# The down projection of a streaming encoder step computed from seven block products instead of eight

## The chip, the cores and the metric

The kernel runs on one core of one Trainium2 chip. The metric is the time of one execution on the device in microseconds (us). The engines are named as in the profile: PE does the matmuls (PEld loads their stationary operands), DVE, ACT and POOL do the work on vectors, SP issues most of the DMAs, and POOL issues some.

## The reference

One step of a one-layer encoder: a mixer of three kinds of recurrent heads, then a feed-forward block with a causal convolution. It works on 1024 prompt rows and 32 sample rows of 1024 features in float32. The change is in the second half:

```python
def conv_ffn(xn, buf, w_up, conv_w, conv_b, w_down):
    up = xn @ w_up                                   # 1024 -> 2 x 2816
    up, buf = causal_dwconv(up, buf, conv_w, conv_b) # width 3
    gate, val = jnp.split(up, 2, axis=-1)
    return (jax.nn.gelu(gate, approximate=True) * val) @ w_down, buf   # 2816 -> 1024
...
h, ffn_buf = conv_ffn(rms_norm(x, g_ffn_pre[l]), ...)
x = x + rms_norm(h, g_ffn_post[l])
```

The product `(gelu(gate) * val) @ w_down` is the down projection: 1056 rows x 2816 features x 1024 outputs. A post norm over the 1024 outputs and the residual follow.

## The kernel before

Every large product is taken in three matmuls of a split operand: `split` (lines 108 to 113) rounds a float32 tile to float32r on ACT (line 110) and takes the remainder on DVE (line 113); `mm3` (lines 103 to 106) adds high x high, high x low and low x high into one PSUM bank. So each operand tile costs one ACT cast and one DVE subtraction, whatever number of matmuls reads it.

The up projection (`up_all`) runs over 22 feature tiles `f` and over two halves `s` of the columns (the rows of the input, 528 columns each). For each it takes seven block products `p1` to `p7` of a 2 x 2 scheme (`up_block`), so it saves one product in eight already. `up_raw` loads the two weight tiles of the next `f` on SP. `up_finish` makes the convolution (POOL copies a few halo columns into `uu`, lines 1335 to 1338; ACT line 1339; DVE line 1341), the gelu (line 1343) and the product with the other half (line 1344), and stores the tile to `h_d[f]` in DRAM (line 1345), 128 features x 1060 columns: 512 prompt rows, two gap columns, 32 sample rows, two gap columns, 512 prompt rows. `uu` is a single pair of buffers. The tile framework orders the instructions of each engine by a timeline of its own and sets the semaphores.

The down projection (`down_all`) takes the 1056 rows in three groups (`DGROUPS`): row blocks 0, 1 and the sample rows (block 8); then 2, 3, 4; then 5, 6, 7. Each group goes over all 22 feature tiles: `load_h` loads the group's columns of `h_d[f]` and all of `w_dn[f]` (512 KB, so the weights are loaded three times) and splits both. Group 0 has the weights stationary and its 288 columns moving (8 banks; the result is turned by PE transposes, line 1460), the others have the rows stationary and 512 weight columns moving. `finish` takes the squares (ACT line 1421), multiplies by the gain (DVE line 1423), gets the reciprocal root on POOL and adds the residual (line 1429) before the store. The last four feature tiles of the last group are held back and done bank by bank, so that the row blocks finish one after the other. `ahead` begins the first two feature tiles of group 0 before the up projection has ended.

PSUM has 8 banks here: four of tag `xw` and one of `sx` in `psf`, three of `big` in `psb`. Split weights live in seven buffers of tag `op`, raw weights in two of tag `raw`.

Of the kernel before, what the change touches and what calls it, by code (L numbers as in the profile page):

```python
# [18 lines left out]
SEQ = 1024  # L19
# [19 lines left out]

DGROUPS = [(0, 1, 8), (2, 3, 4), (5, 6, 7)]  # L40

# [53 lines left out]
def body(ctx: ExitStack, tc: tile.TileContext, a: dict):  # L95
# [45 lines left out]
    h_d = dr.tile([NF, 128, NCOL], F32, name="h_d")  # L141

# [1076 lines left out]

    def up_raw(f):  # L1220
        res = []
        for j in (f, NF + f):
            r = praw[0].tile([128, 1024], F32, tag="raw", name=f"wu{j}r", bufs=2)
            sp.dma_start(r, a["w_up"][j].rearrange("p k n -> p (k n)"))
            res.append(r)
        return res
# [102 lines left out]
    def up_finish(py, f, uu):  # L1329

        ys = []
        for i, j in enumerate((f, NF + f)):
# [5 lines left out]
            pool.tensor_copy(fhalo[:, j, :], u[:, NCOL - 2:NCOL])  # L1338
# [8 lines left out]
    def up_all(pw_, W0, X, uus, py, ahead, begun):  # L1347

        raw, W = {}, {0: W0}
        late = None  # L1350
        for f in range(NF):
# [3 lines left out]
            for s in range(2):  # L1355
# [23 lines left out]
    praw = []  # L1379

    def load_h(ph, g, f, spans, w, deep=None):
        r = ph.tile([128, 384], F32, tag="hr", name=f"hr{g}_{f}", bufs=2)
        for (c0, c1, o) in spans:
            sp.dma_start(r[:, o:o + c1 - c0], h_d[f, :, c0:c1])
        hh = ph.tile([128, 384], F32R, tag="hh", name=f"hh{g}_{f}", bufs=4)
        hl = ph.tile([128, 384], F32R, tag="hl", name=f"hl{g}_{f}", bufs=4)
        split(hh[:, :w], hl[:, :w], r[:, :w], dve)
        wr = praw[0].tile([128, 1024], F32, tag="raw", name=f"wd{g}_{f}r", bufs=2)
        sp.dma_start(wr, a["w_dn"][f])
        return hh, hl, [weight_halves(f"wd{g}_{f}{hf}", wr[:, 512 * hf:512 * hf + 512], deep) for hf in range(2)]  # L1390

    def spans_of(us):
        spans, off, w = [], {}, 0
        for u in us:
            n = 128 if u < 8 else DEC
            off[u] = w
            if spans and spans[-1][1] == fcol(u):
                spans[-1][1] += n
            else:
                spans.append([fcol(u), fcol(u) + n, w])  # L1400
            w += n
        return spans, off, w

    def down_all(ph, p6, gp, begun):
        xres = {}

        def residual(u):
            n = 128 if u < 8 else DEC
            x = p6.tile([128, 1024], F32, tag="xres", name=f"fr{u}", bufs=4)
            sp.dma_start(x[:n], x2_d[128 * u:128 * u + n, :])  # L1410
            xres[u] = x

        def finish(u, n, src):

            x = xres.pop(u)
            ss = p6.tile([128, 4], F32, tag="fss", name=f"gss{u}", bufs=4)
            jk = p6.tile([128, 1024], BF16, tag="fjk", name=f"gjk{u}", bufs=2)
            ys = []
            for hf in range(2):
                c = slice(512 * hf, 512 * hf + 512)  # L1420
                act.activation(jk[:n, c], src[hf], AF.Square, accum_out=ss[:n, 2 + hf:3 + hf])  # L1421
                y = p6.tile([128, 512], F32, tag="yt", name=f"yt{u}{hf}", bufs=4)
                dve.tensor_tensor(y[:n], src[hf], gp[:n, c], op=ALU.mult)
                ys.append(y)
            pool.tensor_tensor(ss[:n, 0:1], ss[:n, 2:3], ss[:n, 3:4], op=ALU.add)  # L1425
            rstd_of(ss[:n, 1:2], ss[:n, 0:1], n, 1, 1024)
            for hf in range(2):
                c = slice(512 * hf, 512 * hf + 512)
                dve.scalar_tensor_tensor(x[:n, c], ys[hf][:n], ss[:n, 1:2], x[:n, c], op0=ALU.mult, op1=ALU.add)
                sp.dma_start(a["yp"][128 * u:128 * u + n, c] if u < 8 else a["ys"][:, c], x[:n, c])  # L1430

        def banks_of(g, m):

            where = [(psf, "xw", 4)] * 4 + [(psb, "big", 3)] * 3 + [(psf, "sx", 1)]
# [330 lines left out]
```

## Time and profile before

| | us |
|---|---|
| median of 3 runs | 1408.08 (1407.53 to 1409.46) |
| the profiled execution's own time | 1407.89 |
| its span, first to last instruction | 1405.9 |
| PE busy | 1364.0 (97%) |
| DVE busy | 1013.9 (72%) |
| ACT busy | 710.8 (51%) |
| POOL busy | 287.9 (20%) |
| mean granted clock of PE | 0.988 of full speed |

A row of a timeline is: start, duration, engine, line, operation, output <- input, shapes, count, and in brackets the idle time of the engine before it and what ended that. A row of instruction groups has the busy time, the mean duration in ns and the idle time before. Matmuls are pipelined: their rows overlap, so their rate is read from start to start and not from durations. Lines L104 to L106 are the three matmuls of `mm3`, and L722 the helper through which the mixer's small products go.

### The profile page before, as it was taken

The page shows a single profiled execution, that of the slowest core. Times are in us where ns is not written, and L with a number is a line of the kernel's source. Part 1 is how long each engine was busy: PE and PEld are TensorE (multiplying, and loading weights), DVE is VectorE, ACT ScalarE, POOL GpSimd, SP SyncE. Part 2 cuts the span into 40 slices and gives each one's busy share as a digit, 9 for nine tenths or more (in the row PEclk, how much of TensorE's full clock was granted, in tenths as well). Part 3 has the DMA queues.
Part 4 walks back from the last instruction along what each step waited for, and adds up shares of the span by engine and source line. Part 5 has one row for each costly group of instructions (what it writes and reads, how often), then busy time and mean ns, then how long its engine had stood idle before and what let it go on. Part 6 is the DMA issues. An engine that isn't in the chain of part 4 may idle for free.

```text
span 1405.9 us, 30168 instructions
## 1 busy us (share of the span) xinstructions
PE 1364.0 (97%) x11804; PEld 1249.8 (89%) x11804; DVE 1013.9 (72%) x1907; ACT 710.8 (51%) x1399; POOL 287.9 (20%) x495
## 2 busy tenths in 40 slices
PE   6999999999999999999899999999999999999998
PEld 5999889898888887777799999999999999988886
DVE  4786468758587669777798888888888865654644
ACT  4556447445474545334755555455545545543432
POOL 5532311235112245212111111111111110000100
PEclk9999999999999989999999999999999999999999
DMA  9599779775789744445312222222122267765752
GB/s 344 191 338 359 259 237 306 230 271 196 270 270 353 249 154 139 142 135 145 124 58 92 97 85 69 84 79 89 62 91 77 74 201 235 242 218 165 252 173 101
DMA packets 129445, 255.11 MB, mean 181 GB/s; under 512 B 27639, under 2 KB 74263, under 8 KB 129303
## 3 DMA queue, kind: packets, MB, share of 16 engines
q1 hardware_dynamic: 122839, 244.54, 52.5%
q10 hardware_dynamic: 4800, 4.33, 0.9%
q0 software_dynamic: 1664, 4.33, 0.8%
q8 instruction: 92, 1.51, 0.4%
q14 instruction: 50, 0.41, 0.1%
HBM read 192.26 MB, written 60.89 MB: 180 GB/s over the span
## 4 chain that ended last, share of the span: by engine, by line
PE 76%; DVE 9%; DMA 7%; ACT 4%; issue 2%; POOL 1%; SPq 0%; ACTq 0%; DVEq 0%; POOLq 0%
PE pd L104 6%; PE pd L105 6%; PE pd L106 6%; PE pux L104 4%; PE pux L105 4%; PE pux L106 4%; PE puw L106 3%; PE puw L104 3%; PE puw L105 3%; PE pv L106 2%; PE pv L104 2%; PE pv L105 2%; PE zp L104 2%; PE zp L106 2%; PE zp L105 2%
## 5 line engine op out<-in xcount | busy, mean ns | idle before, releaser
L1341 DVE SCALAR_TENSOR_TENSOR y<-uu,fconv_sb,y 128x1060 f32<-128x1060 f32 x88 | 116.2, 1321 | 25.0 <-ACT y L1339 24.3
L105 PE MATMUL pd<-wd,hh 128*128 128x512 f32 x264 | 104.3, 395 | 0.0
L104 PE MATMUL pd<-wd,hh 128*128 128x512 f32 x264 | 104.1, 396 | 0.0
L106 PE MATMUL pd<-wd,hl 128*128 128x512 f32 x264 | 104.0, 395 | 0.0
L1277 ACT COPY c<-pux 128x272 f32<-128x272 f32 (+1 forms) x132 | 49.2, 375 | 41.3 <-PE pux L106 37.6
L1339 ACT ACTIVATE y<-uu,fconv_sb 128x1060 f32<-128x1060 f32 x44 | 56.2, 1276 | 17.1 <-POOL uu L1335 16.5
L104 PE MATMUL pv<-wt_0h,xh 128*128 128x256 f32 (+2 forms) x195 | 57.8, 296 | 5.5 <-ACT xh L323 4.5
L104 PE MATMUL zp<-woh,ch 128*128 128x512 f32 (+1 forms) x144 | 58.9, 411 | 1.9 <-DVE z L1158 1.2
L105 PEld LDWEIGHTS pd<-wd,hh 128*128 128x128 f32 x264 | 49.5, 187 | 12.0
L106 PEld LDWEIGHTS pd<-wd,hl 128*128 128x128 f32 x264 | 49.5, 187 | 12.0
L104 PEld LDWEIGHTS pd<-wd,hh 128*128 128x128 f32 x264 | 49.5, 188 | 11.9
L106 PE MATMUL zp<-woh,cl 128*128 128x512 f32 (+1 forms) x144 | 57.6, 401 | 0.2 <-DVE cl L1054 0.2
L105 PE MATMUL zp<-wol,ch 128*128 128x512 f32 (+1 forms) x144 | 57.6, 400 | 0.0
L106 PE MATMUL pv<-wt_0h,xl 128*128 128x256 f32 (+2 forms) x195 | 56.7, 291 | 0.4 <-DVE xl L324 0.4
L106 PE MATMUL pv<-wt_1h,xl 128*128 128x256 f32 (+2 forms) x195 | 57.0, 292 | 0.0
L105 PE MATMUL pv<-wt_1l,xh 128*128 128x256 f32 (+2 forms) x195 | 56.8, 291 | 0.0
L104 PE MATMUL pv<-wt_1h,xh 128*128 128x256 f32 (+2 forms) x195 | 56.7, 291 | 0.0
L105 PE MATMUL pv<-wt_0l,xh 128*128 128x256 f32 (+2 forms) x195 | 56.2, 288 | 0.1
L1338 POOL COPY fhalo<-uu 128x2 f32<-128x2 f32 x44 | 17.6, 399 | 186.7 <-DVE uu L1282 186.7
L1425 POOL TENSOR_TENSOR gss<-gss 128x1 f32<-128x1 f32 (+1 forms) x9 | 2.2, 246 | 244.2 <-ACT gjk L1421 244.2
L104 PE MATMUL pd<-hh,wd 128*128 128x288 f32 x176 | 51.9, 295 | 0.0
L105 PE MATMUL pd<-hl,wd 128*128 128x288 f32 x176 | 51.9, 295 | 0.0
(1680 smaller groups left out, 5213.1 us busy)
## 6 DMA issues: line engine op xcount, KB each, us to landing
h_d<-y SPq DMA_DIRECT2D x22, 530.0 KB, 3.1
wt_0r<-in_w_tok SPq DMA_DIRECT2D x21, 512.0 KB, 5.3
wt_1r<-in_w_tok SPq DMA_DIRECT2D x21, 512.0 KB, 6.7
wt_0l<-lt_d SPq DMA_DIRECT2D x14, 512.0 KB, 3.9
wt_1l<-lt_d SPq DMA_DIRECT2D x14, 512.0 KB, 6.1
hr<-h_d SPq DMA_DIRECT2D x44, 128.0 KB, 3.4
hr<-h_d SPq DMA_DIRECT2D x22, 192.0 KB, 3.5
x<-in_xp SPq DMA_DIRECT2D x8, 512.0 KB, 8.8
```

What stands on the lines that cost most here:

```text
L104: pe.matmul(ps, lh[0], rh[0], start=first, stop=False, **kw)
L105: pe.matmul(ps, lh[0], rh[1], start=False, stop=False, **kw)
L106: return pe.matmul(ps, lh[1], rh[0], start=False, stop=last, **kw)
L1277: kept[name] = act.copy(t, ps)
L1338: pool.tensor_copy(fhalo[:, j, :], u[:, NCOL - 2:NCOL])
L1339: act.activation(y, u, AF.Identity, scale=fconv[:, j, 2:3], bias=fconv[:, j, 3:4])
L1341: dve.scalar_tensor_tensor(y, uu[i][:, s:s + NCOL], fconv[:, j, s:s + 1], y, op0=ALU.mult, op1=ALU.add)
L1425: pool.tensor_tensor(ss[:n, 0:1], ss[:n, 2:3], ss[:n, 3:4], op=ALU.add)
```

## The change

The 1024 prompt rows are cut into two halves, the 22 feature tiles into two halves of 11 (`NP`), the 1024 outputs into two halves. The four blocks of each factor and their sums give seven products `P1` to `P7` (Winograd's form), each over 11 feature pairs `p` with 512 rows, 128 features and 512 outputs a step: four row blocks x three matmuls of 512 columns. The products run in the order P2, P1, P4, P6, P5, P7, P3, in alternation in four banks `W` (`sx` and `big`) and four banks `X` (`xw`). Results are gathered in the SBUF tiles `CA` and `CB`.

- The row tiles `hts[f]` are loaded whole, once, and stay in SBUF, three of them (`EARLY`) during the last half tile of the up projection (`freed`), the others one or two with each step of P2 and one with each of P1 (`rows_of`). Their sums are taken in place on DVE (`combine`, `second_sum`, `fourth_sum`).
- The four sums of weight blocks are taken during the up projection in DRAM, in `ws_d`: 48 copies (`sum_weights`) of up to two feature tiles, 24 plain ones issued by SP behind the latest loads of up weights, and 24 that add to what is there, issued by POOL behind the latest `fhalo` copy. A sum's adding copy comes several copies after the one that it adds to.
- P1 and P2 load a whole tile of `w_dn` and split both halves, of which the product reads the first; the other products load one half or a sum, two feature tiles at a time.
- The 32 sample rows are multiplied in float32 (not split) from the raw tiles, during P2 and P1: with every second step four products (two feature tiles x two output halves) into four quarters of 32 partitions of one bank. Two products with a selection matrix `sel` add the quarters and bring them to the first 32 partitions.
- The gain's second half is negated, which gives the sign of one output half.
- One feature pair is begun ahead of the up projection's end, instead of two feature tiles.
- The last four pairs of P3 are held back and done bank by bank; the upper row blocks (4 to 7) are finished during P3's first steps.

The diff, cut to its core (the removed functions are printed above):

```diff
+    ws_d = dr.tile([4, 128, NF // 2, 512], F32, name="ws_d")
...
-            sp.dma_start(r, a["w_up"][j].rearrange("p k n -> p (k n)"))
+            behind["SP"] = sp.dma_start(r, a["w_up"][j].rearrange("p k n -> p (k n)"))
...
-            pool.tensor_copy(fhalo[:, j, :], u[:, NCOL - 2:NCOL])
+            behind["POOL"] = pool.tensor_copy(fhalo[:, j, :], u[:, NCOL - 2:NCOL])
...
                     next(late, None)
+                    if f == NF - 1 and s == 1:
+                        freed()
+                    m = (2 * f + s - 3) * len(SUMS) // 34
+                    while len(summed) < min(m, len(SUMS)):
+                        sum_weights(*SUMS[len(summed)])
+                        summed.append(m)
...
+    def sum_weights(t, n, q):
...
+        ta, tb, tc_, td = (ws_d[i, :, q:q + n] for i in range(4))
+        dst, x = ((ta, src(0, 0)), (tb, src(0, 1)), (ta, src(0, 1)), (tb, src(1, 1)), (tc_, ta),
+                  (tc_, src(1, 1)), (td, tc_), (td, src(1, 0)))[t]
+        plain = t in (0, 1, 4, 6)
+        with tc.issue_after(behind["SP" if plain else "POOL"].ins):
+            if plain:
+                sp.dma_start(dst, x)
             else:
+                pool.dma_start(dst, x, accum_op=ALU.add)
+    SUMS = [(t, min(2, NP - 2 * i), 2 * i) for _, t, i in
+            sorted((2 * i + 3 * t, t, i) for i in range((NP + 1) // 2) for t in range(8))]
...
+    def down_raw(kind, p):
...
+        turn[0] ^= 1
+        r = (ph[0] if turn[0] else praw[0]).tile([128, 2, 512], F32, tag="raw", name=f"wr{kind}_{p}", bufs=2)
...
+    def load_h(pool_, f):
+        hts[f] = pool_.tile([128, NCOL], F32, name=f"ht{f}")
+        with tc.issue_after(behind["SP"].ins):
+            sp.dma_start(hts[f], h_d[f])
...
+    ASRC = dict(P1=(0, 0), P2=(0, 1), P4=(1, 1), P6=(0, 0), P5=(1, 1), P7=(1, 0), P3=(0, 1))
...
+    def down_operands(ph, kind, p, early=False):
+        down_raw(kind, p)
+        h = halves_of(ablk(*ASRC[kind], p), f"{kind}h{p}", ph, "hop", 4)
+        wp = (ph, "hop", 4) if early else (praw[1], "op", 7)
+        if kind in ("P1", "P2"):
+            r = wraws[kind, p]
+            w = [halves_of(r[:, j], f"{kind}w{p}{j}", *wp) for j in range(2)]
+        else:
+            w = [halves_of(wraws[kind, p // 2][:, p % 2], f"{kind}w{p}", *wp)]
+        return h, w
+    def sample_products(ps, k, p):
+        for q in range(p - p % 2, p + 1):
+            for j in range(2):
+                r = 64 * (q % 2) + DEC * j
+                pe.matmul(ps[r:r + DEC], hts[q + NP * k][:, SMP:SMP + DEC], wraws["P2" if k else "P1", q][:, j],
+                          start=q < 2, stop=q >= NP - 2)
...
+        def run(kind, banks, first, last, each=None, n_end=0):
+            end = []
+            for p in range(NP):
+                ops = begun.pop((kind, p), None) or down_operands(ph, kind, p)
...
+                for i in range(4):
+                    c = slice(128 * i, 128 * i + 128)
+                    mm3(banks[i], (h[0][:, c], h[1][:, c]), wi, first and p == 0, last and p == NP - 1, skip_group_check=True)
+                if each:
+                    each(p, w)
+            return end
...
+        def rows_of(k, bank):
+            def each(p, w):
+                if p % 2 or p == NP - 1:
+                    sample_products(bank, k, p)
+                if k:
+                    for f in (NP + EARLY + p, p - NP + 6):
+                        if 0 <= f < NF and f not in hts:
+                            load_h(ph if f >= NP else ssp, f)
+                elif p + 6 < NP:
+                    load_h(ssp, p + 6)
...
+        run("P2", W, True, True, rows_of(1, s1))
...
+        run("P1", X, True, False, rows_of(0, s2))
...
+            pe.matmul(o[:DEC], sel[:, DEC * j:DEC * j + DEC], keep, start=True, stop=True)
...
+        run("P4", W, True, True, lambda p, w: combine(p))
...
+        close(8, DEC, y8, xs8, ss8)
+        second_sum(0)
+        run("P6", X, False, False, lambda p, w: p + 1 < NP and second_sum(p + 1))
...
+        run("P5", W, True, True, lambda p, w: fourth_sum(p))
...
+        run("P7", X, False, True)
...
+            dve.tensor_tensor(CB[:, i, 0], CB[:, i, 0], X[i], op=ALU.add)
+            dve.tensor_tensor(CB[:, i, 1], X[i], CB[:, i, 1], op=ALU.subtract)
...
+        end = run("P3", W, True, True, each, 4)
...
+    def freed():
+        pxs.close()
+        ph.append(phs.enter_context(tc.tile_pool(name="ph", bufs=1, side="left")))
+        down_raw("P2", 0)
+        for f in range(NP, NP + EARLY):
+            load_h(ph[0], f)
     def ahead():
+        for p in range(1):
+            begun["P2", p] = down_operands(ph[0], "P2", p, True)
```

More of the change, by code (lines that the diff above doesn't have):

```diff
@@ L1392, in spans_of @@
[L1392 to L1398, printed above, removed]
-            else:
[L1400 to L1424, printed above, removed]
@@ new lines, in down_all @@
+        W = w_banks("q5")
+        run("P5", W, True, True, lambda p, w: fourth_sum(p))
+        for i in range(4):
+            act.copy(CB[:, i, 1], W[i])
+            dve.tensor_tensor(CA[:, i, 1], CA[:, i, 1], W[i], op=ALU.subtract)
+        run("P7", X, False, True)
+        late.close()
+        px_ = late.enter_context(tc.tile_pool(name="p12", bufs=1, side="right"))
+        xres = {}
+        for u in (4, 5, 6, 7, 0, 1, 2, 3):
+            xres[u] = px_.tile([128, 1024], F32, name=f"fr{u}")
+            sp.dma_start(xres[u], x2_d[128 * u:128 * u + 128, :])
```

203 lines of the change are left out of this document (123 added, 80 removed).

## The prediction

> **What bounds the kernel now.** I read the page's busy line first, then the windows from the up projection to the end, then the timelines around the places that the change touches. Columns of the windows: length, then busy time and (x instructions) of PE, PEld, DVE, ACT, POOL, granted clock, DMA share, GB/s.
>
> ```profile
> PE 1364.0 (97%) x11804; PEld 1249.8 (89%) x11804; DVE 1013.9 (72%) x1907; ACT 710.8 (51%) x1399; POOL 287.9 (20%) x495
> 707.00:1140.00 433.00, 432.91 (x3549) 432.70 (x3548) 360.78 (x598) 223.53 (x388) 63.99 (x169) 1.00 0.24 82
> 1140.00:1156.00 16.00, 16.00 (x124) 16.00 (x123) 11.86 (x17) 7.59 (x12) 2.06 (x3) 1.00 0.89 279
> 1156.00:1212.00 56.00, 56.00 (x422) 56.00 (x422) 32.36 (x58) 28.78 (x58) 0.00 (x0) 1.00 0.76 235
> ...
> 1399.60:1405.90 6.30, 0.00 (x0) 0.00 (x0) 2.11 (x3) 0.69 (x2) 0.94 (x3) 0.77 0.22 83
> ```
>
> From 707 us on PE never waits, at full clock. DVE is at 83% in the up projection (360.78 of 433 us) and at 58% in the down projection (32.36 of 56), and DMA has most room in the up projection. So a product taken out of the down projection shortens the run, if its operands still arrive; the last 6.3 us are the tail of the last row block.
>
> **The products removed.** Now there are 528 matmuls of 288 columns and 792 of 512.
>
> ```profile
> L105 PE MATMUL pd<-wd,hh 128*128 128x512 f32 x264 | 104.3, 395 | 0.0
> L104 PE MATMUL pd<-hh,wd 128*128 128x288 f32 x176 | 51.9, 295 | 0.0
> 1299.64 0.40 PE L105 MATMUL pd<-wd,hh 128*128 128x512 f32 x1
> ...
> 1302.91 0.40 PE L104 MATMUL pd<-wd,hh 128*128 128x512 f32 x1
> 1140.26 0.30 PE L104 MATMUL pd<-hh,wd 128*128 128x288 f32 x1
> 1140.39 0.30 PE L105 MATMUL pd<-hl,wd 128*128 128x288 f32 x1
> ...
> 1141.86 0.28 PE L104 MATMUL pux<-T3h,S_21h 128*128 128x256 f32 x1
> ...
> 1143.28 0.29 PE L104 MATMUL pd<-hh,wd 128*128 128x288 f32 x1
> 1217.84 0.87 PE pt L1460 x8
> ```
>
> The rows overlap (395 ns each), so I count starts: 14 starts in 1302.91 - 1299.64 = 3.27 us, or 0.2336 us for 512 columns; 0.13 us for 288. The down projection starts at 1140.26 and its matmuls end at 1399.6: 259.3 us, with 1.4 us of interleaved up products (1141.86 to 1143.28) and three times 0.87 us for turning group 0. After: seven products x 11 feature pairs x 12 matmuls = 924 of 512 columns, 924 x 0.2336 = 215.8 us. By this alone the change saves about 42 us. What it gives back follows.
>
> **Sample rows.** 44 float32 matmuls, stationary 128x32, moving 128x512, in sets of four in four column quarters (per factor five sets of four and one of two: 12 sets).
>
> ```profile
> 365.31 0.29 PE L106 MATMUL pf<-xh,wf_8l 128*128 128x288 f32 x1
> 365.53 0.75 PE L548 MATMUL z<-r_fm,wg_sb 16*128 16x288 f32 x2
> 369.14 0.42 PE L722 MATMUL mi<-v,kt 128*32 128x64 f32 x12
> 587.60 0.39 PE L105 MATMUL zp<-wol,ch 128*128 128x512 f32 x1
> 587.92 0.27 PE L722 MATMUL mi<-ident,mqk 64*128 64x64 f32 x1
> 588.13 0.50 PE L106 MATMUL zp<-woh,cl 128*128 128x512 f32 x1
> 588.47 0.39 PE L104 MATMUL zp<-woh,ch 128*128 128x512 f32 x1
> ```
>
> The one product z is two records (x2): float32 is two passes. A 288-column float32r row lasts 0.29 us with 0.13 us between starts, so 0.16 us is latency; z's two passes stream for 0.75 - 0.16 = 0.59 us, about twice 2 x 0.13. So a 512-column pass is 2 x 0.2336 = 0.47 us and a sample product 0.93 us. Do quarters overlap? Twelve passes of 64 columns in 128*32 tiles would need 12 x 0.058 = 0.70 us in a row and take 0.42 - 0.16 = 0.26 us: three to four at a time. Going into another tile shape and back: one small product stretches 587.60 to 588.47, 0.87 us where two starts take 0.46, so at most 0.41 us, of which I take 0.36 as the switch. A set is 0.93 + 0.36 = 1.3 us, 12 sets 15.6 us. One after the other they cost 44 x 0.93 + 12 x 0.36 = 45 us: the other end. I take the low end, for the 128*32 row is the same tile shape.
>
> The Trainium skill's TensorE: Matmul & The Clock Gate (Part 3, measured speedup) gives three column tiles 2.38x. At that efficiency four would give an estimated 3.2x and a set 1.5 us; the sum would be 3 us higher.
>
> Then the halves are added (DVE), turned by two float32 products in one quarter (2 x 0.93 + 0.36 = 2.2 us), and PE waits for the DVE add (0.69 us by the L1423 row below, 1.4 us with an estimated 0.35 us for each of two hand-overs), since product four's first bank is the one that they use.
>
> **Operands per feature pair.** A pair lasts 12 x 0.2336 = 2.8 us on PE.
>
> ```profile
> 1057.02 0.69 DVE L113 TENSOR_TENSOR S_18h<-wu40r,S_18h 128x512 fp32r<-128x512 f32 x1
> 1057.62 0.69 DVE L1248 TENSOR_TENSOR wu18r<-wu40r,wu18r 128x512 f32<-128x512 f32 x1
> 1149.14 1.14 ACT L110 CAST wd<-wd_4r 128x512 fp32r<-128x512 f32 x2
> 1397.62 0.69 DVE L1423 TENSOR_TENSOR yt<-pd,gp 128x512 f32<-128x512 f32 x1 [0.27 <-ACT gjk L1421]
> 1395.94 1.41 DVE L1429 SCALAR_TENSOR_TENSOR fr<-yt,gss,fr 128x512 f32<-128x512 f32 x2 [0.49 <-POOL gss L223]
> ```
>
> A DVE operation of 512 columns takes 0.60 us from start to start, a cast on ACT 0.57. P2 and P1 still split the second weight half, which nothing reads: 3 x 0.60 = 1.8 of 2.8 us, free under PE. P4 has two splits and two row differences, 2.4 us, plus 2.4 us for the CA additions and about 3 us for the sample rows' finish: 32 us beside 31 of PE. Operands run up to three pairs ahead, so P4 itself loses nothing, but P6's first rows queue behind that finish: 2 us. P5, P6, P7 are below 2 us a pair. P3: eight CB additions, four upper row blocks at 2 x 0.60 + 1.41 us, four squares' products and the remaining seven pairs at 1.2 us give 4.8 + 10.4 + 2.4 + 8.4 = 26 us, then four times 2.6 us at the end: 36.4 us against 30.8 of PE and a tail of 7.3. The two nearly coincide; I take 2 us. The tail is 6.3 us and one DVE addition with its hand-over, 1 us. The other four changes of product find their banks already read: 0.5 us each, 2 us.
>
> **Start of the down projection.** Only one pair is begun ahead (2.8 us of PE) where two tiles of 24 matmuls were (6.4 us). DVE had 11.86 of 16 us to do at 1140 to 1156, mostly the last feature tile's convolution, and three splits a pair come to it. No cover is left: 3 us, between 0 and the 6.4 us.
>
> **Loads.** P2 loads 11 weight tiles of 512 KB and 14 row tiles of 530 KB, 13.4 MB in 31 + 8 = 39 us, 345 GB/s. The trace moved 279 GB/s at a share of 0.89, or 313 at a full share: 43 us. Three row tiles and one weight tile come before, so I take 2 us (0 to 15, rival three). The Trainium skill's DMA: Bandwidth & Descriptors (Specifications) puts a core's limit at about 358 GB/s, with which P2 would just fit: 2 us less.
>
> **Weight sums in the up projection.** 24 plain copies on SP, 24 adding copies from POOL, 512 KB each, some 25 MB in 350 us, 72 GB/s beside 82 at a share of 0.24: there is room even if an adding copy costs double. Each SP copy stands behind a pair of up loads, which have slack: wu19 is issued at 1060.81 and first used at 1070.35.
>
> ```profile
> 1050.51 0.33 SPq L1345 DMA_DIRECT2D h_d<-y  x1
> ...
> 1060.81 0.33 SPq L1224 DMA_DIRECT2D wu19r<-in_w_up  x1
> 1071.00 0.33 SPq L1345 DMA_DIRECT2D h_d<-y  x1
> 1070.35 0.62 ACT L110 CAST A_19h<-wu19r 128x512 fp32r<-128x512 f32 x1 [2.43 <-PE puy L106]
> L434 POOL DMA_DIRECT2D g_d<-vg x36: 537/582/792, 127.8 to 531.3; - x36
> 1063.76 0.19 POOL L1338 COPY fhalo<-uu 128x2 f32<-128x2 f32 x1 [3.53 <-DVE uu L1282]
> 1064.07 1.30 POOL L1335 COPY uu<-uu 128x2 f32<-128x2 f32 x1
> 1065.40 1.27 ACT L1339 ACTIVATE y<-uu,fconv_sb 128x1060 f32<-128x1060 f32 x1 [0.56 <-POOL uu L1335]
> ACT y L1339 <- POOL uu L1335: 16.5, 22, 2.2
> ```
>
> POOL is where it can hurt: the adding copies are queued behind the fhalo copy, and right behind that stands the uu copy for which ACT's y waits. An issue is 0.58 us. Behind a waiting adding copy stand all uu copies; but the copy that it adds to was issued several half tiles before (a tile's period is 1071.00 - 1050.51 = 20.5 us), so it should not wait. 24 x 0.58 = 14 us is the upper end if each delay reached PE, 0 the lower; y's users have some slack, and I take 1 us.
>
> **Sum.** From 1140.3: 1.4 up products + 215.8 + 15.6 + 2.2 + 1.4 + 2 (P6) + 2 (other changes) + 3 (start) + 2 (loads) + 2 (P3) + 7.3 (tail) = 254.7, span 1395.0; with 1 us in the up projection 1396.0. The profiled execution took 1407.89 us for a span of 1405.9, 2.0 us around it, and lies 0.2 us under the median of 1408.08: 1398.0 us.
>
> **Rivals.** One: the quarters don't overlap, because the scheduler puts float32r matmuls between them or different moving rows exclude each other. 45 - 15.6 = 29 us more: 1427. Against it stands the 128*32 row. It makes the run slower once a set takes over 2.1 us. Two: the adding copies hold up the uu copies and the up projection stretches, each time by an issue of 0.79 us, the longest seen: 24 x 0.79 = 19 us, 1416. It decides from 10 / 24 = 0.4 us per copy. For it: uu is one buffer, and ACT already waits there 22 times; against it: DVE is idle for 17% there, and the longest of those waits, 2.2 us, cost PE nothing. Three: loads bind P2: at the 235 GB/s of 1156 to 1212, 13.4 MB take 57 us, 15 to 18 more than PE, and the run ends at 1413; the share of 0.76 there, with PE fully busy, says that 235 was demand and not a limit.
>
> **Chances.** Forecast 0.70, with a range of its own of 1386 (start, loads, P6, the other changes, P3 and the up projection at nothing, 12 less) to 1408 (start at 6.4, sets 3 more, 4 in the up projection); rivals 0.08, 0.12 and 0.10. About 0.2% (2.8 us) is what can be told from no change here. Of the forecast 0.06 lies within that, of rival three 0.02; so faster 0.64, same 0.08, slower 0.28. The range takes in rivals two and three and leaves out one: 1386 to 1417.
>
> **What would show it.** Right: 924 products at 0.23 us starts; sample passes in fours, 1.3 us a set; up period still 20.5 us; PE gaps of 1 to 3 us at P2's start, before P4, before P6 and nowhere else. Wrong: up period over 21 us with waits on POOL uu; PE waiting on DMA for ht or wr in P2; DVE over 95% in P4 or P3 with PE idle beside it.

## The result and the profile after

The changed kernel takes 1404.97 us (median of 20 runs, 1401.84 to 1409.88) against 1409.27 us of the kernel before (20 runs beside it). The ratio is 0.997, with a 95% interval of 0.9959 to 0.998: faster, by 4.3 us, where the prediction had 10. The direction was right and the time lies in the range, but more than half of the gain is missing.

The profiled execution took 1408.66 us for a span of 1406.9 us, 3.7 us above the median. Executions differ ahead of the change: the first matmul of the up projection lay between 661.9 and 668.7 us in the profiled executions of kernels that are alike up to there. So stages are compared by their lengths below, not by the times at which they end.

The first line of the page after, then the windows of the profile after, cut at the stages. The columns are those of the windows in the prediction: length, busy time of PE, PEld, DVE, ACT and POOL, granted clock, DMA share, GB/s.

```profile
PE 1355.1 (96%) x11476; PEld 1208.4 (86%) x11476; DVE 1047.4 (74%) x1947; ACT 718.1 (51%) x1393; POOL 321.2 (23%) x519
```

```profile
668.70:1143.84 475.14, 468.03 (x3758) 463.48 (x3756) 390.59 (x633) 252.34 (x445) 88.96 (x209) 1.00 0.47 133
1143.84:1187.96 44.12, 44.12 (x185) 26.48 (x185) 30.27 (x47) 24.70 (x42) 2.03 (x3) 1.00 0.94 356
1187.96:1230.96 43.00, 42.40 (x181) 25.98 (x179) 25.86 (x42) 20.01 (x37) 0.00 (x0) 1.00 0.57 195
1230.96:1238.45 7.49, 3.53 (x6) 0.54 (x5) 7.49 (x14) 4.62 (x9) 0.00 (x0) 0.65 0.39 125
1238.45:1362.46 124.01, 124.01 (x529) 99.67 (x529) 80.40 (x130) 57.42 (x104) 1.85 (x3) 0.99 0.38 118
1362.46:1393.40 30.94, 30.94 (x133) 24.55 (x131) 25.18 (x43) 13.52 (x35) 17.20 (x12) 1.00 0.29 111
1393.40:1406.90 13.50, 0.05 (x1) 0.00 (x0) 9.67 (x16) 2.60 (x8) 6.42 (x12) 0.64 0.42 155
```

The rows are the up projection, P2, P1, the gap between P1 and P4, the four products P4 to P7, P3, and the tail. PE is busy through all the products, which is what the prediction did not expect: it had waits of 1 to 3 us at P2's start, in P2, before P6 and in P3. The down projection lasts 1406.9 - 1143.84 = 263.1 us; the prediction had 254.7. Three places hold the excess.

First, the sample products. PE's timeline in P1:

```profile
1196.44 1.05 PE L1461 MATMUL s<-wrP,ht 128*32 128x512 f32 x4
1197.42 1.20 PE L101 MATMUL x<-P1w,P1h 128*128 128x512 f32 x4
...
1200.42 1.05 PE L1461 MATMUL s<-wrP,ht 128*32 128x512 f32 x4
...
1225.92 1.07 PE L1461 MATMUL s<-wrP,ht 128*32 128x512 f32 x8
1226.92 0.50 PE L101 MATMUL x<-P1w,P1h 128*128 128x512 f32 x1
```

A product has two records, so x4 is a visit of two products (one feature tile) and x8 a set of four. From one visit to the next pass 1200.42 - 1196.44 = 3.98 us with twelve matmuls in between, 12 x 0.2336 = 2.80 us, so a visit costs 1.18 us. The set of four at 1225.92 occupies 1.00 us where the visit of two occupies 0.98. Two visits at P2's start hold a single product and occupy 0.97 us (1143.84 to 1144.81, and 1145.71 to 1146.68). The price is one for each visit, hardly for each product. The program asks for 12 sets; the order in which PE runs them has 20 visits, 11 in P2 and 9 in P1, 15 of them of one tile.

Second, the gap between P1 and P4. The timeline, and below it the windows of the same microseconds:

```profile
1229.89 1.28 DVE L1563 TENSOR_TENSOR ca<-ca,x 128x512 f32<-128x512 f32 x2
1229.92 1.05 PE L1461 MATMUL s<-wrP,ht 128*32 128x512 f32 x4
...
1232.89 0.69 DVE L1563 TENSOR_TENSOR ca<-ca,x 128x512 f32<-128x512 f32 x1
...
1233.49 0.70 DVE L110 TENSOR_TENSOR P4w<-wrP,P4w 128x512 fp32r<-128x512 f32 x1
1234.09 0.70 DVE L1554 TENSOR_TENSOR keep<-keep,s 128x512 f32<-128x512 f32 x1
...
1234.93 3.59 PE L1558 MATMUL so<-keep,sel 128*32 128x512 f32 x4 [3.96 <-DVE keep L1554]
...
1238.45 0.80 PE L101 MATMUL q<-P4w,P4h 128*128 128x512 f32 x1
```

```profile
1231.00:1235.00 4.00, 0.07 (x1) 0.10 (x2) 4.00 (x8) 3.16 (x6) 0.00 (x0) 0.78 0.50 166
1235.00:1238.40 3.40, 3.40 (x4) 0.43 (x4) 3.40 (x7) 1.43 (x4) 0.00 (x0) 0.50 0.28 77
1238.40:1240.50 2.10, 2.10 (x7) 1.68 (x7) 2.10 (x4) 1.31 (x3) 0.17 (x1) 0.60 0.71 199
```

The sums of the sample rows are complete at about 1231. The add that the selection products need starts at 1234.09, because DVE first runs adds into CA, sums and differences of rows for P4 and P7, and a split, in its order. PE is idle for 3.96 us, and the granted clock falls to 0.50 in the stretch behind that: the four passes take 3.52 us (1234.93 to 1238.45), and P4 starts slowly.

Third, the tail: 13.5 us in this window, 13.4 behind the end of the last matmul, where the prediction had 7.3.

```profile
1392.36 1.09 PE L103 MATMUL q<-P3w,P3h 128*128 128x512 f32 x4
1392.79 2.48 DVE L1615 TENSOR_TENSOR ca<-ca,q 128x512 f32<-128x512 f32 x4 [5.76 <-PE q L103]
...
1401.44 2.08 DVE L1522 SCALAR_TENSOR_TENSOR fr<-ca,gss,fr 128x512 f32<-128x512 f32 x3 [0.44 <-POOL gss L221]
```

The four last matmuls of the four banks stand in one row (x4): the banks end together. DVE waited 5.76 us for them and then has all four lower row blocks to finish.

### The profile page after: what moved, and what is told of

Its sections match the earlier page's. It is cut to its first block, busy times and chain, and to the rows that moved or that the text cites. A ratio compares the mean times of both kernels' runs of the same rounds, so it can differ in the third digit from the quotient of the medians.

```text
span 1406.9 us, 29277 instructions
## 1 busy us (share of the span) xinstructions
PE 1355.1 (96%) x11476; PEld 1208.4 (86%) x11476; DVE 1047.4 (74%) x1947; ACT 718.1 (51%) x1393; POOL 321.2 (23%) x519
## 4 chain that ended last, share of the span: by engine, by line
PE 76%; DVE 9%; DMA 7%; ACT 4%; issue 2%; POOL 1%; SPq 0%; POOLq 0%; DVEq 0%; ACTq 0%
PE pux L102 4%; PE pux L101 4%; PE pux L103 4%; PE q L101 3%; PE q L102 3%; PE puw L102 3%; PE pv L101 3%; PE puw L103 3%; PE puw L101 3%; PE pv L103 3%; PE q L103 3%; PE pv L102 3%; PE mi L720 2%; PE zp L101 2%; PE zp L103 2%; PE zp L102 2%
## 5 line engine op out<-in xcount | busy, mean ns | idle before, releaser
L1338 POOL COPY fhalo<-uu 128x2 f32<-128x2 f32 x44 | 17.5, 397 | 181.5 <-DVE uu L1282 181.5
L1518 POOL TENSOR_TENSOR gss<-gss 128x1 f32<-128x1 f32 (+1 forms) x9 | 7.8, 871 | 220.5 <-ACT gjk L1514 134.1
L220 POOL TENSOR_SCALAR hrs<-hss 128x5 f32<-128x5 f32 (+3 forms) x27 | 9.8, 364 | 163.1 <-DVE hss L922 161.7
L431 POOL TENSOR_TENSOR vg<-vth,gh 128x256 f32<-128x256 f32 (+1 forms) x36 | 30.6, 850 | 63.8 <-DMA vm<-v_d 22.4
L1335 POOL COPY uu<-uu 128x2 f32<-128x2 f32 x44 | 34.4, 781 | 45.0 <-DVE uu L1282 44.1
L101 PEld LDWEIGHTS pv<-wt_0h,xh 128*128 128x128 f32 (+1 forms) x195 | 36.9, 189 | 5.6 <-ACT xh L321 4.9
L851 DVE TENSOR_TENSOR Qz<-x,qe 128x128 f32<-128x128 f32 (+1 forms) x106 | 29.9, 300 | 12.8 <-PE sc L720 12.0
L815 DVE COPY_PREDICATED P<-masks_sb,sc 128x352 f32<-128x352 int32 (+1 forms) x44 | 29.8, 676 | 12.4 <-PE sc L720 12.2
L103 PEld LDWEIGHTS pv<-wt_0h,xl 128*128 128x128 f32 (+1 forms) x195 | 36.9, 189 | 1.2 <-DVE xl L322 0.9
L103 PEld LDWEIGHTS pv<-wt_1h,xl 128*128 128x128 f32 (+1 forms) x195 | 36.9, 189 | 0.6 <-issue 0.2
```

The lines of the kernel that those rows point to most:

```text
L101: pe.matmul(ps, lh[0], rh[0], start=first, stop=False, **kw)
L103: return pe.matmul(ps, lh[1], rh[0], start=False, stop=last, **kw)
L431: pool.tensor_tensor(o[:n], th[:n], gh[:n, c0:c0 + 256], op=ALU.mult)
L815: dve.copy_predicated(dst, mk.broadcast_to([n, 11, *mk.shape[2:]]), src)
L851: dve.tensor_tensor(Qp[:, 2 * i, :, :n // 2].rearrange("p e (m c) -> p e m c", c=c), second(x4[:, f:f + 1], c).broadcast_to([128, 2, n // ...
L1335: pool.tensor_copy(u[:, GAP_P:GAP_P + 2], u[:, GAP_S - 2:GAP_S])
```

## Experiments

Two groups of theories stood against each other. The first: a visit has a fixed price and there are more of them than meant; the gap is a matter of DVE's order; the tail comes from the order of P3's last pairs. The rivals: the sample products cost by number, or rows ready late; DVE, the loads or the adding copies are what is really full, so that a cured place only moves its wait. The table has the medians and, from the profiled execution of each kernel, the length of each stage in us, from the matmul that begins it to the one that begins the next (P1 to the end of its last matmul or set); the last column goes from the first matmul of the down projection to the end.

| kernel | median us (runs) | visits | P2 | P1 | to P4 | P4 to P7 | P3 | tail | whole |
|---|---|---|---|---|---|---|---|---|---|
| changed kernel | 1404.97 (20) | 20 | 44.1 | 43.0 | 7.5 | 124.0 | 31.0 | 13.4 | 263.1 |
| whole sets | 1401.14 (9) | 12 | 45.2 | 38.0 | 4.7 | 123.3 | 31.0 | 13.4 | 255.6 |
| bank by bank | 1402.96 (12) | 20 | 44.1 | 43.0 | 6.7 | 123.3 | 33.5 | 9.6 | 260.3 |
| add first | 1400.02 (9) | 20 | 44.1 | 43.0 | 4.9 | 123.9 | 31.0 | 13.4 | 260.3 |
| the three together | 1400.52 (8) | 12 | 47.0 | 38.0 | 3.9 | 123.3 | 33.5 | 9.8 | 255.5 |
| few sample products | 1385.16 (4) | 4 | 36.3 | 37.0 | 0 | 123.2 | 31.0 | 13.4 | 240.8 |
| no weight sums | 1405.06 (10) | 20 | 44.1 | 43.0 | 8.0 | 123.9 | 31.0 | 13.4 | 263.4 |
| sets, lighter P2 | 1397.94 (6) | 12 | 44.6 | 38.0 | 5.9 | 123.8 | 31.0 | 13.4 | 256.7 |
| selection in P6 | 1396.71 (6) | 20 | 44.1 | 43.0 | 0 | 125.3 | 31.0 | 13.4 | 256.8 |
| no unused splits | 1397.04 (4) | 18 | 46.5 | 40.2 | 1.8 | 123.3 | 31.0 | 13.4 | 256.2 |
| sets, five raw tiles | 1399.44 (7) | 12 | 43.2 | 38.0 | 5.5 | 123.3 | 31.0 | 13.4 | 254.3 |
| combined | 1395.64 (6) | 12 | 45.4 | 38.0 | 0 | 125.3 | 31.0 | 13.4 | 253.1 |
| combined, bank by bank | 1394.94 (6) | 12 | 43.9 | 38.0 | 0 | 125.3 | 33.5 | 10.5 | 251.1 |

Each ratio below is to the kernel before, run beside it (1409.17 to 1409.66 us). Medians of 4 to 12 runs here are uncertain by 2 to 4 us either way (the intervals below), so small steps are read from the stages. The stages are those of one execution each, and the granted clock alone moves them: behind 2.92 us of idle time the gap of whole sets has four selection passes of 0.45 us each, and behind 2.99 us that of the lighter P2 has slower ones, 2.88 us for the four, so that the same order gives a gap of 4.7 and of 5.9 us.

### Whole sets

```diff
+                with tc.issue_after(step[0].ins):
+                    step[0] = pe.matmul(   # each sample product behind the one ahead,
+                                           # the first behind the last matmul of its step
```

> The sample-row products are chained behind the last matmul of their step, so that the four quarters of two feature tiles stay together: 12 visits where the changed kernel makes 20 to 21 (most of them of one tile, two products). Theory (a visit to the 32-column tiles has a fixed price of 1.16 us, whether it holds two products or four): 8 to 9 visits fewer, 9 to 10 us off the changed kernel's 1404.97 us, so about 1395.5; DVE's part and the tail stay, so the steps of P2 and P1 alone become shorter. Rival (the price is per product, four quarters take twice what two take): 44 products as before, within 1 us of 1405. Second rival (PE waits for the second tile's row of samples, since a set can only start with its later tile): 12 visits, but gaps in front of each, 2 to 5 us saved.

Measured: 1401.14 us, ratio 0.9949 (0.9931 to 0.9967). The windows of P2, P1 and the gap:

```profile
1139.75:1184.95 45.20, 40.42 (x191) 26.29 (x189) 30.37 (x47) 25.35 (x43) 1.43 (x3) 1.00 0.88 342
1184.95:1222.95 38.00, 38.00 (x178) 25.21 (x176) 26.66 (x43) 19.53 (x38) 0.00 (x0) 1.00 0.57 211
1222.95:1227.68 4.73, 1.81 (x5) 0.36 (x4) 4.73 (x9) 3.16 (x6) 0.00 (x0) 1.00 0.72 258
```

P1 fell by 5.0 us with three visits fewer and without the 0.6 us wait and the handful of P2 matmuls mixed into it; it now holds nothing but 132 x 0.2336 + 6 x 1.2 = 38.0 us. P2 has five visits fewer and is not shorter: PE is now idle for 45.20 - 40.42 = 4.8 us in it: 1.8 us at the start, where the prediction had 3, and 3.0 us in three places behind that, where it had 2 for loads. In the changed kernel the early visits of single tiles stood at the start. What waits for what in P2 (us in total, times, longest):

```profile
SPq L1419 <- PE s L1464: 17.4, 5, 5.0
ACT P2w L107 <- DMA wrP<-in_w_dn: 7.3, 6, 1.9
PE q L101 <- ACT P2w L107: 3.6, 4, 1.4
```

The issue of weight loads waits five times for a set, the casts wait for the loads, and PE waits for the casts; in the changed kernel the casts of P2's weights waited 0.9 us for loads. The theory was right for P1 and wrong for P2. The 3.8 us between the medians lie in the second rival's range, but PE waits for the casts of weights, and not for sample rows in front of each set.

### Bank by bank

```diff
+                with tc.issue_after(fin[0].ins) if fin else ExitStack():
+                    m = mm3(W[i], ...)      # a bank's last pairs behind the bank ahead
```

> The last four feature-tile pairs of the last block product are held in the order written: all of one bank, then the next bank, so that three of the four row blocks can be finished while PE still multiplies. Theory (the tail after the last matmul is long because the scheduler deals the pairs over all four banks, so all four end together): the tail goes from 13.6 us to 7.5 to 8.5, 5 to 6 us off the changed kernel's 1404.97, about 1399.5. Rival (the tail is bound by the engines that finish the rows, ScalarE's squares, POOL's sums and DVE's products, which take some 3 us a block whatever the order): the tail falls to 11 or 12 only, 2 us saved. Everything ahead of the last block product stays as it is.

Measured: 1402.96 us, 0.9964 (0.9945 to 0.9983). Windows of P3 and the tail, and two places of its timeline:

```profile
1355.90:1389.40 33.50, 31.72 (x133) 24.30 (x131) 29.88 (x49) 15.62 (x41) 9.10 (x19) 1.00 0.30 116
1389.40:1399.00 9.60, 0.00 (x0) 0.00 (x0) 5.26 (x9) 0.72 (x2) 3.38 (x6) 0.66 0.44 164
```

```profile
1376.52 0.75 DVE L1522 SCALAR_TENSOR_TENSOR fr<-cb,gss,fr 128x512 f32<-128x512 f32 x1
1377.19 0.69 DVE L110 TENSOR_TENSOR P3h<-ht,P3h 128x512 fp32r<-128x512 f32 x1
1377.79 0.75 DVE L1522 SCALAR_TENSOR_TENSOR fr<-cb,gss,fr 128x512 f32<-128x512 f32 x1
1377.93 0.50 PE L103 MATMUL q<-P3w,P3h 128*128 128x512 f32 x1 [1.12 <-DVE P3h L110]
```

The tail fell by 3.8 us, and P3 gave back 2.5: to multiply the last pairs bank by bank all four of them must be split before, and DVE has the upper row blocks (fr) between those splits. Together 43.1 us for 44.4. The time is the rival's, 2 us in the median, but not its tail: 9.6 us lies between the theory's 8 and the rival's 11. The last bank's add into CA starts 1.3 us behind the last matmul, since DVE still finishes the row blocks ahead of it (1389.36 to 1390.64). The prediction's 2 us of waits for P3 was near for this order: PE is idle for 1.8 us.

### Add first

```diff
+        kept["keep"] = dve.tensor_tensor(keep, keep, s2, op=ALU.add)
+        with tc.issue_after(kept["keep"].ins):   # the adds into CA and the row differences
```

> On DVE the four adds into the accumulator and the row-block differences of the next product are held behind the one add that the selection products wait for. Theory (in the changed kernel this add stands behind four adds, three sums and a split, and PE is idle 3.96 us for it): the idle time falls to about 1 us, 3 us off the changed kernel's 1404.97, about 1402. Rival (DVE's work is only put off: the split of the fourth product's weights then comes late and PE waits as long ahead of that product or the one behind it): within 1 us of 1405.

Measured: 1400.02 us, 0.9944 (0.9927 to 0.9961); the gap is 4.9 us for 7.5, P4 to P7 as long as before. The theory held in direction, against the rival; of its 3 us of idle time 1.9 went (2.05 for 3.96), and the four passes took 2.8 us for 3.5. The add is still not first: a split of P4's weights stands ahead of it and starts at 1229.49, when its cast on ACT is done, 0.6 us behind the end of the sums. The clock fell here as well, behind an idle time of 2.05 us only; with five raw tiles (below) 3.65 us of idle time left it whole:

```profile
1228.90:1230.90 2.00, 0.00 (x0) 0.00 (x1) 1.41 (x3) 2.00 (x4) 0.00 (x0) 1.00 0.57 145
1230.90:1233.70 2.80, 2.77 (x4) 0.42 (x4) 2.80 (x6) 2.20 (x6) 0.00 (x0) 0.64 0.30 121
```

```profile
1219.50:1223.00 3.50, 0.00 (x0) 0.00 (x0) 3.50 (x7) 1.66 (x3) 0.00 (x0) 1.00 0.89 324
1223.10:1224.90 1.80, 1.77 (x4) 0.35 (x4) 1.80 (x4) 0.68 (x2) 0.00 (x0) 1.00 0.03 14
```

### The three together

The edit is the three above.

> The three edits together: sets of four kept together, the last block product ended bank by bank, the add ahead of the selection products first on DVE. Theory (the three excesses over the forecast lie one after another on PE's path, so they add): 9 + 5.5 + 3 = 17.5 us off, about 1387.5, under the forecast of 1398 because the 11 us of waits that the forecast counted aren't there. Rival (each edit moves DVE's work together, and a new wait in front of the fourth block product takes some back): 1392 to 1395.

Measured: 1400.52 us, 0.9939 (0.9915 to 0.9963). A miss by 13 us in the time and by 10 in the stage, 255.5 us where 263.1 - 17.5 = 245.6 was expected: P2 waits instead of visiting (47.0 us), P3 gives back 2.5 us, and the gap is cured twice. P2 is 1.8 us longer than with whole sets alone because the granted clock was at half for one stretch of it (PE is busy for 42.1 us in P2 where it was for 40.4):

```profile
1150.01:1153.42 3.41, 3.41 (x10) 2.63 (x9) 2.02 (x6) 1.56 (x2) 0.85 (x2) 0.50 0.12 41
```

But this is the kernel whose order the prediction had assumed, twelve whole sets, the add in time, the last pairs bank by bank, and its down projection takes 255.5 us; the prediction's sum was 254.7. The terms agree less than the sum: 6.6 us of waits for 11, a tail of 9.8 us for 7.3, and the half clock, which had no term.

### Few sample products

```diff
-                if p % 2 or p == NP - 1:
+                if p == 1:
                     sample_products(bank, k, p)
```

> Only the sample-row products of the first two feature tiles of each factor are made, the other 36 are left out (the sample rows of the output are then not the reference's): 2 to 4 visits where the changed kernel makes 20 to 21. Theory (a visit costs 1.16 us on PE's path wherever it stands): 17 to 18 visits fewer, 20 us off the changed kernel's 1404.97, about 1385. Rival, from the look at the kernel with whole sets, where taking nine visits out of both products let only the second of them (P1) become shorter by their price: in the first (P2) the loads set the pace and hide the visits, so that only P1's nine visits are saved, 10.5 us, and 1 to 4 us in P2, about 1391.5.

Measured: 1385.16 us, 0.9827 (0.981 to 0.9845). P2 and P1:

```profile
1140.13:1176.48 36.35, 35.22 (x150) 25.77 (x150) 29.11 (x46) 24.30 (x42) 2.03 (x3) 1.00 0.98 374
1176.48:1213.34 36.86, 36.25 (x149) 25.91 (x148) 28.20 (x46) 24.60 (x47) 1.69 (x3) 1.00 0.86 312
```

The time that the first theory gave came out, in two parts. 16 visits fewer, 18.9 us at 1.18, made P2 and P1 87.1 - 73.2 = 13.9 us shorter; in the other direction P1 holds the selection products here, 1.8 us and a switch, and P2 has 1.1 us of idle time. With these added back 17.1 us remain for 16 visits, 1.07 us each; the other 1.8 us are not accounted for. The rest is the gap of 7.5 us, which is gone, since the sums are complete long before P1 ends, and the slow start of P4. So the visits cost nearly their price in P2 as well (8 fewer, 7.8 us and 1.1 us of idle time), against the rival. The loads that P2 needs go through in 36.35 us, at 374 GB/s, with 1.1 us of idle time: the loads alone are not what makes P2 wait in the kernels with whole sets.

### No weight sums

```diff
-                    while len(summed) < min(m, len(SUMS)):
-                        sum_weights(*SUMS[len(summed)])
-                        summed.append(m)
```

> The 48 copies that make the weight sums in DRAM are left out, and the products P4 to P7 read plain weight blocks of the same size (the output is then not the reference's). Theory (the copies run on queues with room while PE is busy, and the stage of 44 feature tiles took 389.0 us with them and 388.1 us without): within 1 us of the changed kernel's 1404.97 in the up projection, all else alike, 1404 to 1405. Rival (the copies on POOL's queue hold up POOL's small copies and stretch every tile): the up projection is shorter by more than 2 us, up to 19.

Measured: 1405.06 us, as fast as the changed kernel. The up projection:

```profile
665.90:1140.30 474.40, 467.81 (x3758) 463.25 (x3756) 391.34 (x633) 251.03 (x445) 70.34 (x185) 1.00 0.24 84
```

474.40 us without the sums and 475.14 with them (the first row of the windows after); the kernel before takes 475.0 us (665.30 to 1140.26). So 0.7 us is what the profiled executions show for 48 copies that raise the DMA share from 0.24 to 0.47.

### Sets, lighter P2

The edit of whole sets, and beside it:

```diff
-                    for f in (NP + EARLY + p, p - NP + 6):
+                    for f in (NP + EARLY + p, p - NP + 4):
...
-        sp.dma_start(gp, ...)     # moved behind P2
```

> The kernel with whole sets, and beside it fewer loads in the first product: the rows of P1's feature tiles are loaded four tiles ahead and not six, so 1.1 MB of them moves out of P2 into P1, and the 0.5 MB of row factors is loaded behind P2. Theory (with whole sets PE waits in P2 for loads, at 375 to 415 GB/s in 1160 to 1190 us): 1.6 MB fewer at 410 GB/s is 3.9 us of transfer, 3 to 4 us off the 1401.14 us of the kernel with whole sets, about 1397.5; the steps of P2 come near to P1's 5.8 us for two tiles plus 1.0 us for the set. Rival (PE waits for the splits on ScalarE and DVE, not for the loads): no change in P2, about 1401.

Measured: 1397.94 us, 0.9926 (0.991 to 0.9941), the time that was expected, but not for the reason given: P2 takes 44.6 us for 45.2, with 4.2 us of idle time for 4.8, and the down projection 256.7 for 255.6. The steps show no 3 us. The amount of loads alone isn't what P2 waits for, and the 3.2 us between the medians stay unexplained.

### Selection in P6

```diff
         run("P1", X, True, False, rows_of(0, s2))
+        kept["keep"] = dve.tensor_tensor(keep, keep, s2, op=ALU.add)   # the adds into CA behind it
-        for j in range(2): ... pe.matmul(o[:DEC], sel[...], keep, ...)
...
-        run("P6", X, False, False, lambda p, w: p + 1 < NP and second_sum(p + 1))
+        run("P6", X, False, False, lambda p, w: rows(p))   # selection at p == 2, its finish at p == 4
```

> The two selection products of the sample rows, and what follows from them, are moved from ahead of the fourth block product P4 into the third step of P6, and the add that they read comes first on DVE; all else is the changed kernel. Theory (between P1 and P4 PE waits 4.55 us and then goes at half speed for some microseconds, 0.85 us a pass where the kernel with whole sets shows 0.43 us): the wait of 4.2 us goes, 1.7 us of the slow passes and some 0.7 us at P4's start, while two passes of 0.43 us each and a visit stay: P1's last set to P4's first matmul goes from 8.5 us to 0.5 us, P6 grows by 2 us, 6 us off the changed kernel's 1404.97, about 1399. Rival (P4's fourth bank holds the sums of the sample rows and comes free only behind the same add, so PE waits there instead): 2 to 3 us off, about 1402.

Measured: 1396.71 us, 0.9915 (0.9898 to 0.9932). Its timeline where P1 ends:

```profile
1222.94 1.05 PE L1461 MATMUL s<-wrP,ht 128*32 128x512 f32 x4
...
1223.92 0.50 PE L101 MATMUL q<-P4w,P4h 128*128 128x512 f32 x1
...
1225.10 0.68 DVE L1554 TENSOR_TENSOR keep<-keep,s 128x512 f32<-128x512 f32 x1
```

P4 starts 0.98 us behind the start of the last visit, and the add runs beside it without anyone waiting. The gap of 7.5 us went, P4 to P7 grew by 1.3: 6.2 us in the stages, as the theory had it.

### No unused splits

```diff
-            w = [halves_of(r[:, j], f"{kind}w{p}{j}", *wp) for j in range(2)]
+            w = [halves_of(r[:, 0], f"{kind}w{p}0", *wp)]
```

> In P2 and P1 the split of the second weight half, which nothing reads, is left out: 22 casts on ScalarE and 22 subtractions on DVE fewer, 13 us of DVE's time. Theory (as the prediction had it: 1.8 of 2.8 us a pair, free under PE): within 1 us of the changed kernel's 1404.97. Rival (DVE stands ahead of the selection products and of P1's first operands, so that less of it brings them forward): 2 to 4 us off.

Measured: 1397.04 us, 0.9926 (0.9898 to 0.9954). This was the surprise: 8 us in the median, 6.9 in the stages. P2 and P1 together are 86.7 us for 87.1, with 18 visits for 20, so the splits left out of them bought nothing there, as the prediction had it. What changed is the end of P1:

```profile
1221.31 1.91 PE L1461 MATMUL s<-wrP,ht 128*32 128x512 f32 x12
...
1223.15 1.19 PE L101 MATMUL x<-P1w,P1h 128*128 128x512 f32 x4
...
1223.91 0.68 DVE L1554 TENSOR_TENSOR keep<-keep,s 128x512 f32<-128x512 f32 x1
...
1226.14 1.90 PE L1558 MATMUL so<-keep,sel 128*32 128x512 f32 x4
```

The last sample products now stand ahead of the last pair's matmuls, the add runs beside these, and the selection products follow without a wait and at full clock (gap 1.8 us for 7.5). The order of the built program came out otherwise. That it did so because fewer splits bring P1's last operands forward, as the rival had it, fits but isn't shown by a run of its own. It is the same gap that the kernel with the selection in P6 closes.

### Sets, five raw tiles

The edit of whole sets, and beside it (the pools and their sizes left out here):

```diff
-        turn[0] ^= 1
+        turn[0] = (turn[0] + 1) % 5      # three raw tiles in one pool, two in the other
```

> The kernel with whole sets, and five raw weight tiles in place of four. Theory (in P2 a set keeps both of its raw tiles until it has run, so the loads behind it go out in pairs and land late; the lighter loads changed nothing in the steps of P2): one tile more lets the next load out a step earlier, 2 to 4 us of P2's waits go, P2 falls from 45.2 us (its first matmul to P1's first) to 42 or 43. Rival (the transfers, at 375 to 415 GB/s, or the splits at P2's start are the limit): P2 stays at 44.5 to 45.5 us, and the run at 1398 to 1401.

Measured: 1399.44 us, 0.9936 (0.9913 to 0.9959). P2 takes 43.2 us for 45.2, with 2.8 us of idle time:

```profile
1138.33:1181.50 43.17, 40.42 (x189) 26.26 (x189) 29.46 (x46) 24.74 (x43) 2.07 (x3) 1.00 0.98 375
```

That speaks for the theory that a set holds its two raw tiles and so puts off the loads behind it. It is one execution. Of the next two kernels, with five raw tiles and more edits beside them, the second has P2 at 43.9 us and the first at 45.4, of which 3.41 us ran at half clock:

```profile
1152.17:1155.58 3.41, 3.41 (x10) 2.63 (x9) 2.46 (x4) 0.62 (x2) 0.00 (x0) 0.50 0.99 357
```

So the fifth tile seems to be worth 1 to 2 us. What sets the idle time that is left in P2, 3 to 4 us, stays open.

### Combined, without and with bank by bank

The edits are whole sets, five raw tiles, the selection in P6 and no unused splits; then the end of P3 bank by bank as well.

> Whole sets, five raw weight tiles, the selection products moved into P6, and the unused splits left out. Theory (the gains lie one after another on PE's path): the 1396.7 us of the kernel with late selection products, less some 5 us for the sets and up to 3 us in P2, 1389 to 1392; the stage from P2's first matmul to the end takes 247 to 250 us, where the changed kernel takes 262.1. Rival (with fewer visits P2 waits as much as it saves): 1394 to 1396.

> The kernel before this one, and the end of P3 bank by bank. Theory (the tail shrinks by 3.6 us and P3 grows by 2.5 us of waits for DVE, as in the kernel that had this edit alone): 1 us less than the kernel without it. Rival (with P3 starting earlier against DVE's work the waits grow): 0 to 3 us more.

Measured: 1395.64 us, 0.9911 (0.9892 to 0.9931), and 1394.94 us, 0.99 (0.9877 to 0.9923). The first expectation was missed by 4 us: P2's waits are back, as its rival had it. The second kernel has the lowest median of those that compute everything, 14.4 us under the 1409.35 us of the kernel before in those runs, though the intervals of the two overlap; its P3 and tail take 44.0 us for 44.4 of the first, so that bank by bank is worth nearly nothing, and the rest of what lies between them is P2 with the half clock of the first. Its windows of P2, P4 to P7, P3 and the tail:

```profile
1137.40:1181.30 43.90, 39.94 (x189) 26.54 (x189) 22.70 (x35) 19.60 (x34) 2.07 (x3) 1.00 0.97 370
...
1219.30:1344.50 125.20, 125.20 (x532) 99.25 (x533) 86.38 (x141) 60.72 (x112) 6.64 (x3) 1.00 0.38 125
1344.50:1378.00 33.50, 31.76 (x133) 24.32 (x131) 29.86 (x49) 15.67 (x41) 9.07 (x19) 1.00 0.29 112
1378.00:1388.50 10.50, 0.00 (x0) 0.00 (x0) 5.49 (x9) 0.72 (x2) 3.05 (x6) 0.73 0.40 150
```

What is left beside 215.8 us of products: 12 visits, the selection, 4.0 us of waits in P2, 1.7 in P3, and the tail.

## Why the prediction was right in sign and wrong in size

**Right: the products removed.** Each of the seven takes 132 x 0.2336 = 30.8 us: P4 to P7 take 124.0 us, four times that and the slow start of P4.

**Right: the weight sums.** Predicted 1 us; the up projection takes 475.1 us with them, 474.4 without and 475.0 in the kernel before. The adding copies hold up nobody: rival two is out.

**Right: the price of a set.** Predicted 1.3 us, measured 1.00 us on PE and 0.2 in the matmuls behind it. The quarters overlap, so the strong form of rival one is out. The row from which the prediction took three to four at a time gives 2.7 (0.70 us of passes in 0.26 us).

**Wrong: the number of visits.** The prediction counted "twelve sets" from the loop in the program. PE runs 20 visits, 23.6 us for 15.6. Half of rival one's mechanism was there, products of the large kind between the quarters of a set, at 1.18 us a visit and not 0.93 us a product. Shown by the kernels with few sample products and, for P1, with whole sets.

**Wrong: the step from the sample rows to P4.** Predicted 1.4 us of wait and 2.2 us of products. The gap is 7.5 us, with some 0.8 us of slow matmuls at P4's start. The prediction let the add run as soon as its data was there and did not ask what stands ahead of it on DVE, and it had no term for the clock. Of the 3.96 us the hand-over from DVE to PE is 0.14 us (the add ends at 1234.79); the rest is DVE's queue and the add. Shown by the kernels with the add first and with the selection in P6.

**Wrong: the tail.** 13.4 us for 7.3. The program writes the last pairs bank by bank; the built order deals them over the four banks. The kernel that holds the written order shows 3.8 of the 6.1 us. It still has 2.3 us more than the sum: 1.3 us of that pass before the last add on DVE, and the rest isn't broken down.

**Wrong the other way: the waits.** Start 3, loads 2, before P6 2, the other changes of product 2, P3 2: 11 us counted, 0.6 us there (P1's row, 43.00 - 42.40). Of these, 6.6 us are real where the written order is kept (4.8 us in P2 with whole sets, 1.8 us of idle time in P3 bank by bank); those before P6 and at the other changes of product appear in no kernel. The built order fills the others with visits and with matmuls of other banks, and pays for it in the visits and in the tail.

**Rival three** (loads bind P2) is out as a mechanism of the changed kernel: PE is busy in all of P2. The Trainium skill's DMA: Bandwidth & Descriptors (Specifications) puts a core's limit at about 358 GB/s, as half of 716 GB/s for two cores; with one core at work the trace differs, with 374 GB/s over P2's 36 us in the kernel with few sample products.

The account: 1.4 (up products) + 215.8 + 20 x 1.18 = 23.6 + 7.5 + 0.8 + 0.6 + 13.4 = 263.1 us, as measured. Against the prediction that is 8.0 for the visits, 4.7 for the gap, 6.1 for the tail and 10.4 less for waits: 8.4 us, of which the medians show 7.0. (With the 0.2 us that its last step names, the prediction's sum gives 1398.2 us and not 1398.0; nothing hangs on it.)

## What to carry to other kernels

Where a scheduler orders the instructions, count visits, waits and tails in the order that it builds, not in the loops as written: here it spent waits that were forecast and bought a longer tail and more switches with them, and the leaving out of work that was free by itself moved the order and was worth 6.9 us. Ahead of a small operation for which the bottleneck engine waits, look up what is queued on its engine, and best move the consumer to where nobody waits. In this kernel a switch of PE into another tile shape costs 1.2 us per visit, with one product in it or four, so put as much into one as the buffers allow, and see which buffers that holds.

## What was not expected of the hardware

Four float32 products in four column quarters take 1.00 us on PE where two take 0.98 and one takes 0.97: all but the first are nearly free. The Trainium skill's TensorE: Matmul & The Clock Gate (Part 3, Measured speedup vs the span model) gives 2.38x for three column tiles; this trace shows no such loss from one to four.

PE's granted clock falls to 0.50 behind a short wait, and the same four selection passes take 3.5 us and not 1.8. It is not the length of the wait alone: ahead of these passes the clock fell behind 3.96 and 2.05 us of idle time and stayed whole behind 3.65, 2.92 and, with the three edits together, 2.08. Ahead of the tail the half clock of the down projection lasts 3.41 us or twice that, and its stretches begin on steps of 3.41 us. Counted within the one step just ahead, PE was idle for 2.3 us in the changed kernel and 2.05 with the add first, where the clock fell, and for 1.97 us at most with five raw tiles, where a wait of 3.65 us lay across two steps. So it matters how a wait falls on the steps. That isn't the whole rule: in P2 the clock fell behind steps with 1.73 us of idle time (the three together) and 1.62 (combined) and stayed behind one with 1.74 (combined, bank by bank).

The Trainium skill's TensorE: Matmul & The Clock Gate (Part 1: The HAM clock gate) has the half rate after an idle window of about 3.4 us that runs freely. The half rate and the steps agree; but in the steps ahead of these falls PE was busy for 1.1 to 1.8 of 3.41 us, so a window need not be idle throughout.
